# Tiles at equal places modulo 2 KB, one 1/rms chain for two row tiles, and the first bias tiles loaded ahead, in a fp32r transformer block

## The chip, the cores and the metric

The kernel runs on one core of one Trainium2 chip. The metric is the device time of one execution in microseconds, as the median of several runs. The core has a tensor engine (TensorE, PE in the profile; its weight loads are PEld), a vector engine (VectorE, DVE), a scalar engine (ScalarE, ACT), GpSimd (POOL) and a queue engine (SyncE, SP) that issues nearly all DMA transfers here, in order. Each engine works through its own instructions in order and waits on semaphores.

## The reference, cut to what matters

One layer of an encoder with 1024 positions and width 1024: attention over chunks, a short convolution, gates, an output projection and an MLP.

```python
h = rms_norm(x, norm1_g)
q, k, v, bg, cg, xc = split(h @ w_in)                     # 6 x 1024 columns
y_attn = attention(rms_norm(q), rms_norm(k), v, rel_bias) @ w_attn_proj   # 16 heads of 64
y_conv = (bg * conv3(cg * xc)) @ w_conv_proj
g_attn, g_conv = split(sigmoid(h @ w_gate + b_gate))
x = x + (g_attn * y_attn + g_conv * y_conv) @ w_out
x = x + square(relu(rms_norm(x, norm2_g) @ w_up)) @ w_down
```

## The kernel before

Every fp32 matrix product is done as three fp32r products: an operand is cut into a high part (ScalarE, a cast) and a low part (VectorE, the difference), and high x high, low x high and high x low are added in PSUM. `split` does the cut. A step of a product is thus three matmuls, mostly with 128x128 stationary tiles and 512 moving columns.

**The start and the first pair of heads.** The positions are eight row tiles of 128. `row_load` fetches a transposed row tile `xt`, `row_cut` multiplies it with the gain and cuts it into `hT` (row tiles 0 to 3 in `hT0`, 4 to 7 in `hT1`). `row_scale` fetches the same rows in the other layout (`xn`), and ScalarE and GpSimd make 1/rms of the rows (`rr`) from them. For head pair `p`, `fetch` and `cut` load and cut four weight tiles (`r_q`, `w_q`); then each row tile takes 24 matmuls into `psq` (q, k and v of two heads, 384 columns). `evac` empties it: ScalarE squares (`sq`), VectorE adds up (`ss`, the reduction), GpSimd makes 1/rms of each head (six small instructions on tile `qw`, the function `rstd` among them), VectorE multiplies (`qn`). The last step is put off by `later(QN[0], ...)`, and so are the values `vt`. After row tile 5, `tr_q` and `tr_k` transpose the first four row tiles of q and k (`tq`, `tk`), cut them (`qh`, `kh`), and copies by DMA make `q` and `k2` of them. In the first pair the `psq` tiles go round eight PSUM banks, three of which `tq` and `tk` use too.

**Attention.** For each pair `unit_stages` makes scores `s` (PSUM), adds the bias tile `b` and finds the largest (L361, VectorE), exponentiates, transposes (`tp`), cuts (`pt`) and multiplies with `vt` (`av`). The next pair's 192 `psq` matmuls are woven in between. `load_bias` fetches a bias tile and masks two corners on GpSimd. The bias tiles lie in pool `a2`, which is opened on the right side of SBUF after `ln1`, the pool of the start, is closed.

**Seven-product jobs.** The gates 4 to 7 of eight, the convolution's projections and the up projection run as jobs of two by two blocks with seven products (`product`, `phase`): each of the seven block products of a job is 4 steps of 3 matmuls with 512 columns, 84 matmuls in a job. There are 16 such jobs before the projections and 16 in the up projection. In each set the first job is "wide" (all seven products for one moving tile after the other), the last is wide too, in the order `leave`; the 14 between are regular: each product goes through its four moving tiles, three matmuls each. The moving tiles are `oh0` to `oh3` and `on0` to `on3`, one after the other.

**Plain stages.** `ps_cp`, `ps_ap`, `ps_o` and `ps_d` (the convolution's and attention's projections, the output projection, and the down projection) are products of 512 columns in PSUM with all weights on the right side of SBUF. Their moving tiles are `yk`, `ak`, `mk` and `uk`.

**SBUF** is given out from two sides: pools by default from the left (low addresses), those with `side="right"` from the right. The left side begins behind a scratch area that the compiler keeps for DMA descriptors.

Of the kernel before, what the change touches and what calls it, by code (L numbers as in the profile page):

```python
# [40 lines left out]
def block_kernel(ctx, tc, x, xt, wqkv, wcnv, wgate, wcp, wap, wout, wup, wdown,  # L41
# [14 lines left out]
    make_identity(nc, ident)  # L56
    ones = const.tile([P, P], F32, name="ones")
    nc.gpsimd.memset(ones[:], 1.0)
    nhalf = const.tile([P, 4], F32, name="nhalf")
    nc.gpsimd.memset(nhalf[:], -0.5)  # L60
    gq8 = const.tile([P, 1], F32, name="gq8")
    nc.vector.tensor_scalar(gq8[:], sv[:, C_GQ:C_GQ + 1], DH ** -0.5, None, op0=ALU.mult)
# [109 lines left out]
    uD = [dram.tile([P, S], F32, name=f"uD{t}") for t in range(FF // P)]  # L172


    def row_load(pool, st, parts=1):
        xg = pool.tile([P, ND, P], F32, name=f"xt{st}", tag="xt", bufs=4)
        n = ND // parts
        for i in range(parts):
            nc.sync.dma_start(xg[:, i * n:(i + 1) * n], xt[st, :, i * n:(i + 1) * n])
        return xg  # L180

    def row_cut(xg, st, parts=1, gated=False):
        so = (st % 4) * P
        h = hT[st // 4]
        n = ND // parts
        for i in range(parts):
            k = slice(i * n, (i + 1) * n)
            g = sv[:, C_G1 + i * n:C_G1 + (i + 1) * n].unsqueeze(2).to_broadcast([P, n, P])
            ins = (nc.vector.tensor_tensor(xg[:, k], xg[:, k], g, op=ALU.mult),)
            ins += split(h[:, 0, k, so:so + P], h[:, 1, k, so:so + P], xg[:, k])  # L190
            if gated:
                for j in ins:
                    gate(j)

    def row_scale(pool, sts):
        n, a = len(sts), sts[0]
        w = pool.tile([P, 4, 4], F32, name=f"rw{a}", tag="rw")
        ss, v, y, t = (w[:, i, :n] for i in range(4))
        for st in sts:
            xn = pool.tile([P, D], F32, name=f"xn{st}", tag="xn")  # L200
            nc.sync.dma_start(xn[:], x[st * P:(st + 1) * P, :])
            nc.scalar.activation(xn[:], xn[:], AF.Square, accum_out=w[:, 0, st - a:st - a + 1])
        nc.gpsimd.tensor_scalar(v, ss, 1.0 / D, EPS, op0=ALU.mult, op1=ALU.add)
        nc.gpsimd.tensor_scalar(rr[:, 1, a:a + n], v, EPS, None, op0=ALU.mult)
        rstd(y, t, v)
        nc.gpsimd.tensor_scalar(t, t, -0.5, 1.5, op0=ALU.mult, op1=ALU.add)
        nc.gpsimd.tensor_tensor(rr[:, 0, a:a + n], y, t, op=ALU.mult)
# [7 lines left out]
    def qkv_stages(p):  # L215
# [39 lines left out]
        def evac(st, ps):  # L255
            hf, s4 = st // 4, st % 4
            qk = ps[:, 0:256].rearrange("p (a b) -> p a b", a=4)
            sq = aw.tile([P, 4, DH], F32, name=f"sq{p}_{st}", tag="sq")
            w = a1.tile([P, 4, 4], F32, name=f"qw{p}_{st}", tag="qw")
            ss, v, y, t = (w[:, i, :] for i in range(4))  # L260
            nc.scalar.square(sq[:], qk)
            nc.vector.tensor_reduce(ss, sq[:], axis=AX.X, op=ALU.add)

            nc.gpsimd.tensor_scalar(v, ss, 1.0 / DH, rr[:, 1, st:st + 1], op0=ALU.mult, op1=ALU.add)
            rstd(y, t, v)
            nc.gpsimd.tensor_scalar(t, t, -0.5, 1.5, op0=ALU.mult, op1=ALU.add)
            nc.gpsimd.tensor_tensor(y, y, t, op=ALU.mult)
            pv = ps[:, 256:384].rearrange("p (h d) -> p h d", h=2)
            vh, vl = c.vt[:, st, :, 0, :], c.vt[:, st, :, 1, :]
            r = rr[:, 0, st:st + 1]  # L270

            def values():
                gate(nc.scalar.activation(vh, pv, AF.Copy, scale=r))
                gate(nc.vector.scalar_tensor_tensor(vl, pv, r, vh.bitcast(F32),
                                                    op0=ALU.mult, op1=ALU.subtract))

            def normed():
                gate(nc.vector.tensor_tensor(
                    c.qn[hf][:, s4].rearrange("p a (h d) -> p (a h) d", h=2),
                    qk, y.unsqueeze(2).to_broadcast([P, 4, DH]), op=ALU.mult))  # L280
# [46 lines left out]
    biast = {}

    def load_bias(p, h):
        if p >= NH // 2:  # L330
            return
        bt = biast[p, h] = a2.tile([P, 5 * P], F32, name=f"b{p}_{h}", tag="bias")
        nc.sync.dma_start(bt[:], biasw[2 * p + h])
        nc.gpsimd.memset(bt[0:64, 576:640], NEG)
        nc.gpsimd.memset(bt[64:128, 0:64], NEG)

    def unit_stages(p, c, m, h):

# [115 lines left out]
            later(n, lambda f=f, u=u: f(u))  # L454


    QN, VN = [7], [7]
    pairs = [qkv_stages(p) for p in range(NH // 2)]
    cur, fetch, cut, tiles, trs = pairs[0]
    with tc.tile_pool(name="ln1", bufs=2) as ln1:  # L460
        xs = {0: row_load(ln1, 0, 2)}
        for u in range(4):
            fetch(u, ln1 if u < 2 else None)
        xs[1] = row_load(ln1, 1)
        row_cut(xs[0], 0, 2)
# [24 lines left out]
        turn[0] = 0  # L490
        banks = [(psmm, "mm")] * 2
# [598 lines left out]
```

## Time and profile before

| | |
|---|---|
| median of 3 runs | 1859.92 us (1859.12 to 1860.83) |
| profiled execution | 1858.92 us, span 1857.1 us |
| TensorE busy | 97% of the span, 8884 matmuls |
| VectorE busy | 61% |
| ScalarE busy | 38% |
| GpSimd busy | 9% |
| mean granted TensorE clock | 0.989 |

The profile is of one execution; its times are microseconds from the first instruction. A busy TensorE is not one at its peak: the matmuls are pipelined, so that a matmul's own duration overlaps the next one's, and how fast they follow each other has to be read from the starts. In a timeline, instructions of one line and tile that follow each other are one row: start, length, and how many (x). What stands in brackets is the engine's idle time before the row and what ended it.

### The profile page before, as it was taken

To read this page: it belongs to the slowest core of one execution; us is meant where nothing else is said; L and a number is where in the kernel's file an instruction comes from. 1 tells how busy PE (TensorE), PEld (TensorE's weight loads), DVE (VectorE), ACT (ScalarE), POOL (GpSimd) and SP (SyncE) were. 2 spreads that over 40 slices of the span, in tenths; PEclk is the share of its full clock that TensorE was granted. 3 is DMA by queue.
4 is the path that set the end of the run, shared out by engine and by line. 5 is a ranking of instruction groups with operands and counts; after the bars stand their busy time and mean duration, and the time that the engine had idled before them with its cause. 6 is when DMAs were issued, how large, how long until landed. Compare 5 with 4: busy or idle time off the path is not lost.

```text
span 1857.1 us, 24757 instructions
## 1 busy us (share of the span) xinstructions
PE 1808.5 (97%) x8884; PEld 1549.0 (83%) x8884; DVE 1124.4 (61%) x2068; ACT 698.2 (38%) x1337; POOL 163.4 (9%) x463
## 2 busy tenths in 40 slices
PE   7899999999999999999999999999999989999998
PEld 6799999999887788888788888788788868888887
DVE  6578787787658766665651528966676451423343
ACT  5455555565433433333341414433333242312210
POOL 5433233222100000000000000000000000000000
PEclk9999999999999899999999999999999999999999
DMA  6433434333425232223583528543233262424232
GB/s 250 117 100 100 104 93 111 103 103 93 115 77 167 80 98 79 63 69 102 187 265 109 178 83 266 190 131 114 94 113 120 91 220 69 131 66 132 68 111 82
DMA packets 123547, 225.02 MB, mean 121 GB/s; under 512 B 13728, under 2 KB 30112, under 8 KB 123424
## 3 DMA queue, kind: packets, MB, share of 16 engines
q1 hardware_dynamic: 123280, 223.40, 39.3%
q8 instruction: 70, 1.15, 0.3%
q14 instruction: 53, 0.43, 0.1%
q10 hardware_dynamic: 144, 0.03, 0.0%
HBM read 147.88 MB, written 50.33 MB: 107 GB/s over the span
## 4 chain that ended last, share of the span: by engine, by line
PE 89%; DVE 4%; DMA 2%; POOL 2%; issue 1%; ACT 1%; SPq 0%; DVEq 0%; ACTq 0%
PE ps_d L74 19%; PE psq L74 12%; PE pa_u L74 8%; PE ps_ap L74 5%; PE ps_o L74 5%; PE ps_cp L74 4%; PE pb_u L74 4%; PE av L74 3%; PE s L74 3%; PE ps_g L74 3%; PE tp L77 3%; PE pa_c L74 2%; PE pa_x L74 2%; PE pa_b L74 2%; PE pc_u L74 2%; PE pa_g L74 1%
## 5 line engine op out<-in xcount | busy, mean ns | idle before, releaser
L74 PE MATMUL psq<-w_q,hT 128*128 128x384 f32 x1536 | 348.6, 352 | 9.9 <-ACT w_q L81 7.3
L74 PE MATMUL ps_d<-uk,w_d 128*128 128x512 f32 x1536 | 351.2, 391 | 6.6 <-DVE uk L82 5.5
L74 PEld LDWEIGHTS ps_d<-uk,w_d 128*128 128x128 f32 x1536 | 289.9, 189 | 67.8 <-DVE uk L82 5.9
L74 PEld LDWEIGHTS psq<-w_q,hT 128*128 128x128 f32 x1536 | 262.8, 193 | 13.6 <-ACT w_q L81 7.3
L74 PE MATMUL pa_u<-on,w_u 128*128 128x512 f32 x672 | 162.9, 394 | 0.0
L74 PEld LDWEIGHTS pa_u<-on,w_u 128*128 128x128 f32 x672 | 126.2, 188 | 29.5 <-issue 0.5
L82 DVE TENSOR_TENSOR w_d<-r_d,w_d 128x512 fp32r<-128x512 f32 x64 | 43.3, 690 | 148.7 <-ACT w_d L81 148.7
L363 ACT ACTIVATE p<-p,sm 128x640 f32<-128x640 f32 (+4 forms) x128 | 89.5, 699 | 83.6 <-DVE sm L361 83.6
L81 ACT CAST w_d<-r_d 128x512 fp32r<-128x512 f32 x64 | 39.2, 623 | 178.5 <-PE ps_d L74 173.3
L74 PE MATMUL ps_g<-hT,w_g 128*128 128x512 f32 x384 | 100.2, 398 | 1.4 <-DVE gp L521 1.4
L74 PE MATMUL ps_cp<-yk,w_cp 128*128 128x512 f32 x384 | 90.4, 398 | 4.5 <-DVE yk L82 3.8
L361 DVE CUSTOM_DVE_ANT_0 p<-s,b 128x640 f32<-128x640 f32 (+4 forms) x128 | 83.4, 652 | 13.7 <-PE s L74 10.4
L74 PEld LDWEIGHTS ps_cp<-yk,w_cp 128*128 128x128 f32 x384 | 73.8, 193 | 20.9 <-DVE yk L82 4.2
L82 DVE TENSOR_TENSOR pt<-tp,pt 128x512 fp32r<-128x512 f32 (+1 forms) x144 | 84.4, 597 | 11.1 <-ACT pt L81 10.5
L74 PE MATMUL s<-k,q 128*128 128x384 f32 (+3 forms) x384 | 82.0, 322 | 6.6 <-DVE sm L361 6.2
L74 PEld LDWEIGHTS av<-pt,vt 128*128 128x128 f32 x576 | 85.5, 188 | 3.2 <-DVE pt L82 1.2
L74 PE MATMUL ps_ap<-ak,w_ap 128*128 128x512 f32 x384 | 88.1, 391 | 0.0
L74 PE MATMUL av<-pt,vt 128*128 128x256 f32 (+1 forms) x576 | 86.7, 272 | 1.0 <-DVE pt L82 1.0
L74 PE MATMUL ps_o<-mk,w_o 128*128 128x512 f32 x384 | 87.3, 389 | 0.0
L81 ACT CAST pt<-tp 128x512 fp32r<-128x512 f32 (+1 forms) x144 | 71.7, 515 | 40.2 <-PE tp L77 40.0
L74 PEld LDWEIGHTS ps_ap<-ak,w_ap 128*128 128x128 f32 x384 | 72.1, 188 | 15.8
L74 PEld LDWEIGHTS ps_o<-mk,w_o 128*128 128x128 f32 x384 | 72.1, 188 | 15.0
(244 smaller groups left out, 2908.6 us busy)
## 6 DMA issues: line engine op xcount, KB each, us to landing
q<-qh SPq DMA_DIRECT2D x128, 128.0 KB, 2.3
r_u_a<-in_wup_dram SPq DMA_DIRECT2D x64, 256.0 KB, 2.7
buk<-uD SPq DMA_DIRECT2D x32, 512.0 KB, 3.7
r_d<-in_wdown_dram SPq DMA_DIRECT2D x64, 256.0 KB, 2.8
r_q<-in_wqkv_dram SPq DMA_DIRECT2D x32, 384.0 KB, 3.4
k<-kh SPq DMA_DIRECT2D x64, 128.0 KB, 2.3
gl<-gD SPq DMA_DIRECT2D x32, 256.0 KB, 3.5
uD<-s_u SPq DMA_DIRECT2D x30, 256.0 KB, 2.0
```

The source lines that it names most:

```text
L74: pin(nc.tensor.matmul(ps, lhsT, rhs, start=start, stop=stop, skip_group_check=chain))
L77: pin(nc.tensor.transpose(o, i, ident[:]))
L81: return (nc.scalar.copy(hi, src), nc.vector.tensor_tensor(lo, src, hi.bitcast(F32), op=ALU.subtract))
L82: nc.vector.tensor_tensor(lo, src, hi.bitcast(F32), op=ALU.subtract))
L361: nc.vector.tensor_tensor_reduce(pw, sc[:, k0:k1], biast[p, h][:, 5 * P - w:], -1.0, 3e38, ALU.add, ALU.min, sm[:, 0:1])
L363: nc.scalar.activation(pw, pw, AF.Exp, bias=sm[:, 0:1], scale=-1.0, accum_out=sm[:, 1:2])
```

## The change

It has three parts.

1. **Places.** The DMA scratch area is set to 1 KB (16 KB before), and a tile `pad` that nothing uses is put on the left side. The built program's addresses, as bytes past a multiple of 2 KB:

| tiles | side | before | after |
|---|---|---|---|
| `hT`, `w_q`, `w_g` 0 to 4, `vt`, `qn` | left | 1568, and steps of 512 | 2016, and steps of 512 |
| `oh1` to `oh3`, `on0`, `on1`, `ak` | left | 1568 | 2016 |
| weights `w` of all later stages | right | 2016, and steps of 512 | the same |
| `oh0`, `on2`, `on3`, `yk`, `mk`, `uk` | right | 2016 | the same |
| `pt` | right | 992 | 992 |
| `q`, `k2` | left | 1696 | 1184 |

2. **One chain for two row tiles.** In the first pair (`p == 0`) `evac` collects the sums of two row tiles in one tile `qw` and runs the chain from `rstd` on once for both, on eight columns. `normed` of the even row tile is put off by eight steps more. `vt` comes nine steps later instead of seven.
3. **Loads and cuts ahead.** The bias tiles of pair 0 move to pool `a1` on the left and are loaded after row tile 2. The loads of the first `xt` and `r_q` alternate in halves, and so do their cuts; the first two `r_q` share the buffers of `xn`.

```diff
-    nhalf = const.tile([P, 4], F32, name="nhalf")
+    nhalf = const.tile([P, 8], F32, name="nhalf")
...
-        raw = (pool or wp[0]).tile([P] + shape, F32, name=f"r_{name}", tag="raw",
-                                   bufs=2 if pool else wp[2])
+        raw = (pool or wp[0]).tile([P] + shape, F32, name=f"r_{name}",
+                                   tag="xn" if pool else "raw", bufs=2 if pool else wp[2])
...
+    const.tile([P, 368], F32, name="pad")
...
+        bt = biast[p, h] = a1.tile([P, 5 * P], F32, name=f"b{p}_{h}", tag="bias")
...
-            w = a1.tile([P, 4, 4], F32, name=f"qw{p}_{st}", tag="qw")
-            ss, v, y, t = (w[:, i, :] for i in range(4))
+            n = 2 if p == 0 else 1
+            b, m = st % n, st - st % n
+            if b == 0:
+                c.qw = a1.tile([P, 3, 4 * n], F32, name=f"qw{p}_{st}", tag=f"qw{n}")
+            w = c.qw
+            ss, v, y = (w[:, i, 4 * b:4 * b + 4] for i in range(3))
...
-            rstd(y, t, v)
-            nc.gpsimd.tensor_scalar(t, t, -0.5, 1.5, op0=ALU.mult, op1=ALU.add)
-            nc.gpsimd.tensor_tensor(y, y, t, op=ALU.mult)
+            if b == n - 1:
+                va, ya, ta = (w[:, i, :] for i in (1, 2, 0))
+                rstd(ya, ta, va)
+                nc.gpsimd.tensor_scalar(ta, ta, -0.5, 1.5, op0=ALU.mult, op1=ALU.add)
+                nc.gpsimd.tensor_tensor(ya, ya, ta, op=ALU.mult)
...
-            later(QN[0], normed)
+            later(QN[0] + 8 * (n - 1 - b), normed)
...
-    QN, VN = [7], [7]
+    QN, VN = [7], [9]
...
-        xs = {0: row_load(ln1, 0, 2)}
-        for u in range(4):
-            fetch(u, ln1 if u < 2 else None)
+        xs = {0: row_load(ln1, 0, 2, lambda i: [fetch(u, None if i else ln1)
+                                                for u in (2 * i, 2 * i + 1)])}
         xs[1] = row_load(ln1, 1)
-        row_cut(xs[0], 0, 2)
-        for u in range(4):
-            cut(u, False)
+        row_cut(xs[0], 0, 2, False, lambda i: [cut(u, False) for u in (2 * i, 2 * i + 1)])
...
+            if st == 2:
+                for h in range(2):
+                    load_bias(0, h)
...
-    for h in range(2):
-        load_bias(0, h)
...
-    nc = _bacc.Bacc("TRN2", target_bir_lowering=False, num_devices=1)
+    nc = _bacc.Bacc("TRN2", target_bir_lowering=False, num_devices=1,
+                     dynamic_dma_scratch_size=1024)
```

How the instructions stand on two engines. VectorE at the start of the program, before (L189 multiplies `xt` with the gain, L82 makes the low part; L262 is the reduction of row tile 0):

```order
L189 TENSOR_TENSOR xt_197<-xt_197,sv 128x512 x2
L82 TENSOR_TENSOR hT_76<-xt_197,hT_76 128x4x128 x2
L82 TENSOR_TENSOR w_q_0_216<-r_q_0_200,w_q_0_216 128x768
L82 TENSOR_TENSOR w_q_1_219<-r_q_1_202,w_q_1_219 128x768
L82 TENSOR_TENSOR w_q_2_222<-r_q_2_204,w_q_2_222 128x768
L82 TENSOR_TENSOR w_q_3_225<-r_q_3_206,w_q_3_225 128x768
L189 TENSOR_TENSOR xt_208<-xt_208,sv 128x1024
L82 TENSOR_TENSOR hT_76<-xt_208,hT_76 128x8x128
L189 TENSOR_TENSOR xt_242<-xt_242,sv 128x1024
```

The same place now (`xt_198` is row tile 0, `xt_209` row tile 1, `xt_243` row tile 2):

```order
L193 TENSOR_TENSOR xt_198<-xt_198,sv 128x512
L82 TENSOR_TENSOR hT_76<-xt_198,hT_76 128x4x128
L193 TENSOR_TENSOR xt_198<-xt_198,sv 128x512
L82 TENSOR_TENSOR w_q_0_214<-r_q_0_200,w_q_0_214 128x768
L82 TENSOR_TENSOR w_q_1_217<-r_q_1_202,w_q_1_217 128x768
L82 TENSOR_TENSOR hT_76<-xt_198,hT_76 128x4x128
L82 TENSOR_TENSOR w_q_2_223<-r_q_2_205,w_q_2_223 128x768
L82 TENSOR_TENSOR w_q_3_226<-r_q_3_207,w_q_3_226 128x768
L193 TENSOR_TENSOR xt_209<-xt_209,sv 128x1024
L193 TENSOR_TENSOR xt_243<-xt_243,sv 128x1024
L82 TENSOR_TENSOR hT_76<-xt_209,hT_76 128x8x128
```

The second half of row tile 0 now stands between the weights, and the low part of row tile 1 has moved behind the product of row tile 2.

GpSimd at the chains of row tiles 2 and 3, before (L264 is the chain's first instruction, L114 its power, L267 its last):

```order
L264 TENSOR_SCALAR qw_3_457<-qw_3_457,rr 128x4
L114 TENSOR_TENSOR qw_3_457<-qw_3_457,nhalf 128x4
L115 TENSOR_TENSOR qw_3_457<-qw_3_457 128x4
L116 TENSOR_TENSOR qw_3_457<-qw_3_457 128x4
L266 TENSOR_SCALAR qw_3_457<-qw_3_457 128x4
L267 TENSOR_TENSOR qw_3_457<-qw_3_457 128x4
```

The same place now (L285 is the old L264, L222 and L223 mask a bias tile, `qw_2_390` holds row tiles 2 and 3):

```order
L222 MEMSET b_0_399 64x64
L223 MEMSET b_0_399 64x64
L285 TENSOR_SCALAR qw_2_390<-qw_2_390,rr 128x4
L114 TENSOR_TENSOR qw_2_390<-qw_2_390,nhalf 128x8
L222 MEMSET b_1_403 64x64
L223 MEMSET b_1_403 64x64
L115 TENSOR_TENSOR qw_2_390<-qw_2_390 128x8
L116 TENSOR_TENSOR qw_2_390<-qw_2_390 128x8
L289 TENSOR_SCALAR qw_2_390<-qw_2_390 128x8
L290 TENSOR_TENSOR qw_2_390<-qw_2_390 128x8
```

One chain on eight columns stands for two on four, and the bias masks have come from behind row tile 7's chain into this one.

VectorE around the first `qn`, now (L297 is the low part of `vt`, L301 is `qn`, `xt_266` is row tile 4 and `xt_259` row tile 3):

```order
L193 TENSOR_TENSOR xt_266<-xt_266,sv 128x1024
L82 TENSOR_TENSOR hT_76<-xt_259,hT_76 128x8x128
L283 TENSOR_REDUCE qw_0_294<-sq_1_342 128x4
L297 SCALAR_TENSOR_TENSOR vt_261<-psq_0_263,rr,vt_261 128x2x64
L82 TENSOR_TENSOR hT_77<-xt_266,hT_77 128x8x128
L301 TENSOR_TENSOR qn_0_262<-psq_0_263,qw_0_294 128x256
L301 TENSOR_TENSOR qn_0_262<-psq_1_298,qw_0_294 128x256
```

Before, `qn` of row tiles 0 and 1 stood ahead of the low part of row tile 4; now both stand behind it.

## Rows read from the trace of the kernel before

**Rows 1.** The page, TensorE: busy us, share of the span, instructions.

```profile
PE 1808.5 (97%) x8884; PEld 1549.0 (83%) x8884; DVE 1124.4 (61%) x2068; ACT 698.2 (38%) x1337; POOL 163.4 (9%) x463
```

**Rows 2.** Timelines of TensorE in `ps_d`, `ps_o`, `ps_ap`: start, length, engine, count.

```profile
1699.62 50.71 PE L74 MATMUL ps_d<-uk,w_d 128*128 128x512 f32 x223
...
1109.69 40.51 PE L74 MATMUL ps_o<-mk,w_o 128*128 128x512 f32 x178
...
1039.80 40.45 PE L74 MATMUL ps_ap<-ak,w_ap 128*128 128x512 f32 x176
```

**Rows 3.** Timelines of TensorE in regular up jobs and in regular convolution jobs.

```profile
1216.78 5.71 PE L74 MATMUL pa_u<-on,w_u 128*128 128x512 f32 x24
...
1255.61 5.71 PE L74 MATMUL pa_u<-on,w_u 128*128 128x512 f32 x24
...
651.05 2.96 PE L74 MATMUL pa_x<-oh,w_x 128*128 128x512 f32 x12
...
695.58 2.96 PE L74 MATMUL pc_x<-oh,w_x 128*128 128x512 f32 x12
```

**Rows 4.** Timelines of TensorE within the last up job, two stretches.

```profile
1475.03 8.32 PE L74 MATMUL p_u<-on,w_u 128*128 128x512 f32 x36
...
1484.35 8.40 PE L74 MATMUL p_u<-on,w_u 128*128 128x512 f32 x36
```

**Rows 5.** Windows: length, then busy us (count) of PE, PEld, DVE, ACT, POOL, clock.

```profile
620.00:880.00 260.00, 260.00 (x1123) 210.90 (x1122) 166.22 (x240) 89.68 (x148) 0.31 (x3) 1.00 0.27 82
1190.00:1468.00 278.00, 274.45 (x1183) 221.50 (x1182) 185.66 (x280) 92.39 (x162) 0.00 (x0) 1.00 0.34 112
...
80.00:560.00 480.00, 478.03 (x3094) 455.39 (x3093) 361.37 (x946) 262.46 (x629) 119.72 (x352) 1.00 0.38 101
```

**Rows 6.** Timelines of TensorE in the first 80 us.

```profile
8.28 19.63 PE L74 MATMUL psq<-w_q,hT 128*128 128x384 f32 x97 [0.30 <-DVE w_q L82]
29.59 6.70 PE L74 MATMUL psq<-w_q,hT 128*128 128x384 f32 x37 [1.69 <-DVE hT L82]
...
42.17 0.47 PE L77 MATMUL tq<-ident,qn 128*128 128x128 f32 x1 [3.99 <-DVE qn L278]
...
44.77 9.73 PE L74 MATMUL psq<-w_q,hT 128*128 128x384 f32 x46 [0.62 <-DVE hT L82]
...
62.91 0.79 PE L74 MATMUL s<-k,q 128*128 128x256 f32 x2 [5.93 <-DVE sm L361]
63.51 5.56 PE L74 MATMUL psq<-w_q,hT 128*128 128x384 f32 x18
```

**Rows 7.** Windows: the stretch after the longest wait (third from the end: granted clock).

```profile
63.40:68.20 4.80, 4.80 (x17) 4.80 (x17) 1.90 (x8) 0.89 (x4) 0.00 (x0) 0.50 0.02 3
```

**Rows 8.** Timeline of all engines in 34 to 75.

```profile
37.51 1.95 POOL L264 TENSOR_SCALAR qw<-qw,rr 128x4 f32<-128x4 f32 x1 [0.89 <-DVE qw L262]
...
41.70 0.42 DVE L278 TENSOR_TENSOR qn<-psq,qw 128x256 f32<-128x256 f32 x1 [2.03 <-POOL qw L267]
...
56.35 0.81 SPq L333 DMA_DIRECT2D b<-in_biasw_dram  x2
...
62.56 0.29 DVE L361 CUSTOM_DVE_ANT_0 p<-s,b 128x128 f32<-128x128 f32 x1 [2.87 <-POOL b L334]
```

**Rows 9.** Groups of GpSimd in 14 to 63: count, busy us, mean ns, idle before.

```profile
L114 POOL TENSOR_TENSOR qw<-qw,nhalf 128x4 f32<-128x4 f32 x8 | 9.0, 1128 | 0.6
L264 POOL TENSOR_SCALAR qw<-qw,rr 128x4 f32<-128x4 f32 x8 | 6.5, 817 | 3.2 <-DVE qw L262 2.7
```

**Rows 10.** Timeline of all engines in 0 to 34.

```profile
4.22 1.35 DVE L189 TENSOR_TENSOR xt<-xt,sv 128x512 f32<-128x512 f32 x2
...
7.52 2.77 ACT L81 CAST w_q<-r_q 128x768 fp32r<-128x768 f32 x3 [0.29 <-DMA r_q<-in_wqkv_dram]
...
8.38 2.90 DVE L82 TENSOR_TENSOR w_q<-r_q,w_q 128x768 fp32r<-128x768 f32 x3 [0.16 <-ACT w_q L81]
...
13.53 1.23 DVE L82 TENSOR_TENSOR hT<-xt,hT 128x1024 fp32r<-128x1024 f32 x1 [1.11 <-ACT hT L81]
```

More of the change, by code (lines that the diff above doesn't have):

```diff
@@ L172, in block_kernel, with row_load @@
     uD = [dram.tile([P, S], F32, name=f"uD{t}") for t in range(FF // P)]
-    def row_load(pool, st, parts=1):
+    def row_load(pool, st, parts=1, then=None):
         xg = pool.tile([P, ND, P], F32, name=f"xt{st}", tag="xt", bufs=4)
@@ L179, in row_load, with row_cut @@
             nc.sync.dma_start(xg[:, i * n:(i + 1) * n], xt[st, :, i * n:(i + 1) * n])
+            if then:
+                then(i)
         return xg
-    def row_cut(xg, st, parts=1, gated=False):
+    def row_cut(xg, st, parts=1, gated=False, then=None):
         so = (st % 4) * P
@@ L193, in row_cut @@
                     gate(j)
+            if then:
+                then(i)
     def row_scale(pool, sts):
@@ L207, in row_scale, with load_bias @@
         nc.gpsimd.tensor_tensor(rr[:, 0, a:a + n], y, t, op=ALU.mult)
+    biast = {}
+    def load_bias(p, h):
+        if p >= NH // 2:
+            return
+        bt = biast[p, h] = a1.tile([P, 5 * P], F32, name=f"b{p}_{h}", tag="bias")
+        nc.sync.dma_start(bt[:], biasw[2 * p + h])
+        nc.gpsimd.memset(bt[0:64, 576:640], NEG)
+        nc.gpsimd.memset(bt[64:128, 0:64], NEG)
     PA = [slice(0, DH), slice(DH, P)]
@@ L325, in skip @@
         pass
[L327 to L335, printed above, removed]
     def unit_stages(p, c, m, h):
```

## The prediction

> **What bounds the kernel now.** I read the page first: TensorE is busy 97% of the span [rows 1], so the time can fall in two ways only: its idle time goes, or its matmuls follow each other faster. The matmuls' own durations overlap and hide the second, so I took TensorE's timeline in stretches without a wait and divided: (length of the merged row − 0.39, the last matmul's own duration) / (count − 1) is the step from one start to the next. All matmuls below are 128x512 fp32r with a 128x128 stationary tile and the same three products per step.
>
> - `ps_d`: (50.71 − 0.39)/222 = 226.7 ns; `ps_o`: (40.51 − 0.39)/177 = 226.7 ns. `ps_ap`: (40.45 − 0.39)/175 = 228.9 ns [rows 2].
> - The seven-product jobs: 14 products of 12 between the two rows of the up projection, 38.83 us/168 = 231.1 ns; 16 products in the convolution's jobs, 44.53/192 = 231.9 ns [rows 3].
>
> The work per instruction is equal, so why three steps? By the table of places above, `ps_d` and `ps_o` read weights and moving tile both at 2016 past a multiple of 2 KB; `ps_ap` reads weights at 2016 and moving tile at 1568; the seven-product jobs read moving tiles that change between 1568 and 2016 every three to nine matmuls. Two other readings would fit so far (the stage, or the seven-product code), so I looked for the same code without the change of side: the last up job (`leave` = 2, 3, 0, 1) reads 42 matmuls from right tiles and then 42 from left ones. The first stretch goes at (8.32 − 0.39)/35 = 226.6 ns, the second at (8.40 − 0.39)/35 = 228.9 ns [rows 4]. Same code, tiles, weights; only the place differs. I take it that equal places give 226.7, unequal ones 228.9, and a change of place now and then some ns more. TensorE is the bound in these stages: in 620 to 880 it is busy all 260 us, VectorE 166; in 1190 to 1468 274 of 278, VectorE 186 [rows 5].
>
> Then the idle time. The first 80 us hold most of TensorE's waits [rows 6]: 1.69 us at 29.59 for `hT`, 3.99 at 42.17 for `qn`, 0.62 at 44.77, 5.93 at 62.91 for `sm`. The two long ones cost twice: after them the granted clock is at its half level (0.50, 1.2 GHz) for 63.4 to 68.2 [rows 7], and the 18 matmuls from 63.51 take 5.56 us, where full speed, 0.176 by the row from 29.59 ((6.70 − 0.35)/36), gives 17 × 0.176 + 0.35 = 3.35.
>
> Who is late there? VectorE runs in order. `qn` at 41.70 waited 2.03 us for GpSimd, whose chain for that row tile began at 37.51 and took L264 alone 1.95 us; only after `qn` comes the next reduction [rows 8]. So each row tile pays reduction, GpSimd chain, `qn` in series. The mean chain is 0.82 + 1.13 for L264 and L114 [rows 9] and four short ones. And 62.91 waits for the bias: its load is issued at 56.35, since its tile takes the place of `ln1`'s last tiles, and VectorE stands 2.87 us until it is masked [rows 8].
>
> **Part by part.**
>
> 1. *Places.* 28 regular seven-product jobs of 84 matmuls, half of them up: 1176 × (231.1 − 226.7) = 5.2 us and 1176 × (231.9 − 226.7) = 6.1 us. The four wide jobs have 42 + 42 + 63 + 63 = 210 matmuls on left tiles: 210 × 2.2 = 0.5. `ps_ap`: 384 × 2.2 = 0.85. Sum 12.7 us, all of it on the path, because VectorE has the room above. Lower bound 0 (the place is not the cause), upper bound 2688 × 5.2 + 0.85 = 14.8 (the wide jobs too). I take 12.7, the stretches being so regular.
> 2. *Attention.* `vt` moves from 1568 to 2016 and so agrees modulo 512 with `pt` at 992, `k2` and `q` with each other as before. No row separates this: TensorE is busy 478.03 of 480 us there over 3094 matmuls [rows 5]. The 576 `av` matmuls could gain at most the 4.4 ns of part 1, 2.5 us; at least, places that now differ elsewhere take back as much, −2.5. I take 0.5.
> 3. *Pair chain.* Two L264, one L114 of eight columns and four short ones replace two whole chains; L114 costs between one of 1.13 and two, 2.26; I take 1.7. VectorE stops once in two row tiles and no longer between `sq` and the next reduction. In the new VectorE order `hT` of tile 4 stands ahead of both `qn`, so the 1.69 goes: 1.7 us. For `tq`: from the start of the wait, 38.18, to the end of tile 7, 54.50, are 16.3 us; the work in it is 48 × 0.176 for tiles 6 and 7 and some 0.6 for five transposes (an estimate: 128 of 384 columns are 0.059, twice that each) = 9.0. Gain 7.3, if the second chain ends before TensorE has done tile 5. Tile 1 counts from 16.05 (part 5), each tile is 24 × 0.176 = 4.2: tile 3 ends at 28.7, its square and reduction at 29.5 (an estimate: two of the 0.42 of `qn`). Then L264 0.82, L114 1.7, the short ones with their gaps 1.1 (41.70 − 37.51 − 1.95 − 1.13) and some 0.6 for four bias masks: 33.7; both `qn` by 34.6; TensorE reaches `tq` at 16.05 + 5 × 4.2 = 37.1. So 2.5 us to spare. Next late are `hT` of tile 6 (34.6 + 0.4 + 1.23 + 1.23 = 37.5, wanted at about 38) and the `q` and `k` copies, for which I find no spare time: up to 1 us of wait.
>    The even tile's `qn` comes eight steps later and holds its bank; the bank is wanted five tiles later, so the matmuls of the tiles between cover it.
> 4. *Bias ahead.* The wait of 5.93 and the slow clock after it go: 5.93 + (5.56 − 3.35) = 8.1 us. What it adds: two loads in SP's queue behind the first two `r_q` of pair 1, and four masks on GpSimd inside the second chain. Behind a mask that waits for its load stand the chain, both `qn`, `tq`. At a late load each us beyond the 2.5 to spare is one of TensorE's.
> 5. *The new start.* The second half of `xt0` now lands behind two weight loads, at about the time that the second of these did, 7.5 [rows 10]. VectorE needs it before `w_q`: 7.5 + 0.68 + 0.97 = 9.15 for the second matmul, against 8.28. Then come `w_q` 1, half of `hT`, `w_q` 2 and 3 (0.97, 0.69, 0.97, 0.97) and, as the order shows, `xt1`, `xt2` and only then `hT` of tile 1 (1.23 each): 16.4 against 13.53 + 1.23 = 14.76. TensorE's tile 1 began at 27.91 − 0.35 − 73 × 0.176 = 14.7 and wants this at its third matmul, 15.05: a loss of 1.3 us. If the loads land earlier than I think it is 0; if `xt2`'s load holds VectorE, some 2.5. The shared `xn` ring makes SP wait for `w_q` 0 (9.15) before `xn0`, and behind it stand `xt2` and the rest; `xn0` feeds a chain that is not wanted before tile 1 is done, so the 4.2 us of tile 1 cover it.
>
> Sum: 12.7 + 0.5 + 1.7 + 7.3 + 8.1 − 1.3 = 29.0 us. The profiled execution took 1858.92, 1.0 below the median of the runs, 1859.92; its span of 1857.1 should become 1828. For the median: **1830.9, I say 1830.5**.
>
> **Rivals.** What this kernel's runs can tell from no change is about 0.2%, 3.7 us.
>
> - *Places do nothing* (the step belongs to the stage). Then part 1 is gone: 1830.5 + 12.7 = 1843. For it: `ps_ap` is another stage than `ps_d`. Against it: the two stretches of one job [rows 4].
>   The Trainium skill, "TensorE: Matmul & The Clock Gate", Part 2 (step ①), has TensorE read the moving tile and the next weights through two independent ports, the load taking nothing from the running matmul. By this rule where the tiles stand would not matter, and the result would be this rival's 1843. The 2.3 ns between the stretches of [rows 4] disagree with it, so it gets a small chance.
> - *The pair chain stalls TensorE again.* In before, L264 took 0.82 on average but 1.95 once. If the chain and the masks take 7 us instead of 4, `tq` waits again, long enough for the half clock, and part 3's 7.3 and perhaps a us of part 4 are lost: 1836 to 1840.
> - *Slower.* The half clock stays. TensorE's start now has one matmul at about 6.5 and then a hole until 9.15, and feeds that are just in time. Each matmul at 1.2 GHz costs (5.56 − 3.35)/17 = 0.13 us more. To eat the 29 us and come out 3.7 slower takes 33/0.13 = 254 of them, more than the first pair's 192; time 1863.6 or more. Against it: the slow stretch from 63.51 ended within 18 matmuls.
> - *Rather more*: no loss at the start, and 2.5 from attention: 1827.
>
> **How the numbers follow.** Both gains as summed, ± 1 us in parts 1 and 2, from −1 to +3 in 3 to 5: 1827.5 to 1834, 68%. Chain stalls: 18%. More: 5%. Places do nothing: 7%. Slower: 1%; nearly no change, from two of these together: 1%. The range of 1825 to 1839 takes in the first, the "more" and most of the stalls. Faster by over 0.2%: 0.97; same 0.01; slower 0.02.
>
> **What would show it.** Part 1: products of the up and convolution jobs start every 2.72 us instead of 2.77 to 2.80, and `ps_ap` merges to 226.7. Part 3: no wait of TensorE on `qn`, none on `hT` over 1.5 us, and a granted clock of 1.00 from 17 us on. Part 4: no wait on `sm` at the second score tile. Part 5: the second matmul at 9.2, and tile 1's third at 16.4. I would be wrong if the products still start every 2.77, if GpSimd's eight-column L114 is well over 2.3 us, or if a mask waits for its load.

## The result, and the profile after

The changed kernel takes 1838.44 us (median of 4 runs, 1836.54 to 1842.08) against 1859.89 before: a ratio of 0.9887, 95% interval 0.9869 to 0.9904, so 21 us faster. The forecast was 1830.5, with a range of 1825 to 1839: the sign and the range hold, the size is 7.9 us short. That the range holds is in part luck: the time lies 0.6 us inside its upper end, and the same kernel run once more took 1840.76 (run 11 below). The profiled execution took 1839.77 us, its span is 1838.0.

Timelines of TensorE in the changed kernel, for [rows 2 to 4]: products of regular convolution and up jobs, `ps_ap`, and the last up job.

```profile
641.73 2.88 PE L74 MATMUL pa_x<-oh,w_x 128*128 128x512 f32 x12
644.45 2.88 PE L74 MATMUL pa_b<-oh,w_b 128*128 128x512 f32 x12
...
999.81 40.51 PE L74 MATMUL ps_ap<-ak,w_ap 128*128 128x512 f32 x178
...
1213.28 2.88 PE L74 MATMUL pb_u<-on,w_u 128*128 128x512 f32 x12
1216.00 2.88 PE L74 MATMUL pa_u<-on,w_u 128*128 128x512 f32 x12
...
1454.40 19.20 PE L74 MATMUL p_u<-on,w_u 128*128 128x512 f32 x84
```

These stages now have one step: 2.72 us for a product of twelve in both sets of jobs, (40.51 − 0.39)/177 = 226.7 ns in `ps_ap`, and (19.20 − 0.39)/83 = 226.6 in the last job, which before fell into a stretch of 226.6 and one of 228.9. This half of the change did what was forecast. The first 80 us did not. TensorE there, for [rows 6], and its granted clock after the two waits, third column from the end, for [rows 7]:

```profile
9.29 7.02 PE L74 MATMUL psq<-w_q,hT 128*128 128x384 f32 x25 [2.04 <-DVE w_q L82]
17.17 20.74 PE L74 MATMUL psq<-w_q,hT 128*128 128x384 f32 x118 [0.85 <-DVE hT L82]
40.58 0.63 PE L77 MATMUL tq<-ident,qn 128*128 128x128 f32 x4 [2.67 <-DVE qn L301]
43.76 1.08 PE L77 MATMUL tk<-ident,qn 128*128 128x128 f32 x4 [2.56 <-DVE vt L297]
44.50 10.52 PE L74 MATMUL psq<-w_q,hT 128*128 128x384 f32 x48
54.85 0.34 PE L74 MATMUL s<-k,q 128*128 128x128 f32 x2
...
56.64 0.40 PE L74 MATMUL s<-k,q 128*128 128x256 f32 x2
```

```profile
44.50:54.80 10.30, 10.30 (x50) 10.30 (x49) 5.61 (x11) 5.15 (x11) 6.74 (x21) 0.80 0.74 171
```

The wait of 5.93 us on `sm` is gone, and so is the one for `hT` of tile 4. But `tq` still waits 2.67 us for `qn`, behind it `tk` waits 2.56 us for `vt`, which nothing had forecast, and then the clock falls: 48 matmuls take 10.52 us where full speed gives 8.6 (run 9 below). The first score starts at 54.85. In the kernel before it started at 54.90:

```profile
54.90 0.42 PE L74 MATMUL s<-k,q 128*128 128x128 f32 x2 [0.40 <-DMA k<-kh]
```

So in these two executions nothing of the start's gain has come by the first score, and all of it comes behind it.

What holds `qn` is seen in the timeline of the other engines, for [rows 8]:

```profile
25.52 0.27 POOL L285 TENSOR_SCALAR qw<-qw,rr 128x4 f32<-128x4 f32 x1
25.87 1.64 POOL L114 TENSOR_TENSOR qw<-qw,nhalf 128x8 f32<-128x8 f32 x1
...
28.68 0.76 DVE L301 TENSOR_TENSOR qn<-psq,qw 128x256 f32<-128x256 f32 x2 [3.31 <-POOL qw L290]
...
29.53 0.37 ACT L296 ACTIVATE vt<-psq,rr 128x128 fp32r<-128x128 f32 x1 [2.65 <-DVE qn L301]
29.68 1.22 DVE L193 TENSOR_TENSOR xt<-xt,sv 128x1024 f32<-128x1024 f32 x1
29.86 1.17 POOL L285 TENSOR_SCALAR qw<-qw,rr 128x4 f32<-128x4 f32 x1 [0.94 <-DVE qw L283]
...
32.17 1.12 POOL L115 TENSOR_TENSOR rw<-rw 128x2 f32<-128x2 f32 x1
32.62 0.38 ACT L282 ACTIVATE sq<-psq 128x256 f32<-128x256 f32 x1
...
34.02 0.41 DVE L283 TENSOR_REDUCE qw<-sq 128x4 f32<-128x256 f32 x1
...
35.74 1.08 POOL L285 TENSOR_SCALAR qw<-qw,rr 128x4 f32<-128x4 f32 x1
...
39.77 0.20 POOL L290 TENSOR_TENSOR qw<-qw 128x8 f32<-128x8 f32 x1
40.01 0.76 DVE L301 TENSOR_TENSOR qn<-psq,qw 128x256 f32<-128x256 f32 x2 [3.31 <-POOL qw L290]
```

Row tile 3 leaves TensorE at 17.17 + 70 × 0.174 = 29.4, but its square (32.62) and reduction (34.02) are late: VectorE stood 3.31 us ahead of the first pair of `qn`, and ScalarE's `vt` of tile 1 waited for that same `qn` (2.65). Behind `vt` on ScalarE stand the cut of a row tile, which waits for VectorE's product from 29.68, and a weight cut, and only then the square. Then GpSimd has the rows' own 1/rms (`rw`) to finish; it takes the second chain up at 35.74, and the chain ends at 39.97.

### The profile page after: what moved, and what is told of

The parts are those of the page before. It is cut to its first block, busy times and chain, and to the rows that moved or that the text cites. A ratio compares the mean times of both kernels' runs of the same rounds, so it can differ in the third digit from the quotient of the medians.

```text
span 1838.0 us, 24737 instructions
## 1 busy us (share of the span) xinstructions
PE 1793.2 (98%) x8884; PEld 1545.9 (84%) x8884; DVE 1124.0 (61%) x2068; ACT 698.1 (38%) x1337; POOL 158.8 (9%) x443
## 4 chain that ended last, share of the span: by engine, by line
PE 90%; DVE 5%; DMA 2%; POOL 1%; issue 1%; ACT 1%; SPq 0%; DVEq 0%; ACTq 0%
PE ps_d L74 19%; PE psq L74 13%; PE pa_u L74 8%; PE ps_ap L74 5%; PE ps_o L74 5%; PE ps_cp L74 4%; PE pb_u L74 4%; PE av L74 3%; PE s L74 3%; PE ps_g L74 3%; PE tp L77 3%; PE pa_c L74 2%; PE pa_b L74 2%; PE pa_x L74 2%; PE pc_u L74 2%; PE p_g L74 1%
## 5 line engine op out<-in xcount | busy, mean ns | idle before, releaser
L82 DVE TENSOR_TENSOR w_d<-r_d,w_d 128x512 fp32r<-128x512 f32 x64 | 43.3, 690 | 148.8 <-ACT w_d L81 148.8
L82 DVE TENSOR_TENSOR pt<-tp,pt 128x512 fp32r<-128x512 f32 (+1 forms) x144 | 84.4, 597 | 10.6 <-ACT pt L81 9.6
```

What stands on the lines that cost most here:

```text
L82: nc.vector.tensor_tensor(lo, src, hi.bitcast(F32), op=ALU.subtract))
```

## The experiments

Since the work after the first pair scatters by some 4 us between the profiled executions (last section), each kernel is also read at one event: the first of the `rb` matmuls, which comes when the start is over. In three profiled executions with the changed kernel's start it came at 82.05, 81.28 and 80.95, so a difference of about 1 us there says nothing.

| kernel | ratio to before, 95% interval | median us | first `rb` matmul |
|---|---|---|---|
| before | | 1859.89 | 90.13 |
| changed | 0.9887 (0.9869 to 0.9904) | 1838.44 | 82.05 |
| 1 places only | 0.9932 (0.9918 to 0.9945) | 1846.91 | 90.18 |
| 2 no places | 0.9959 (0.9946 to 0.9971) | 1851.96 | 83.19 |
| 3 `vt` at seven | 0.9891 (0.9877 to 0.9904) | 1839.31 | 79.49 |
| 4 `qn` later | 0.9883 (0.9870 to 0.9897) | 1837.52 | 80.31 |
| 5 pad 512 less | 0.9889 (0.9874 to 0.9904) | 1841.39 | 81.28 |
| 6 places and bias | 0.9907 (0.9892 to 0.9921) | 1843.60 | 86.23 |
| 7 single chain | 0.9898 (0.9881 to 0.9914) | 1842.35 | 85.76 |
| 8 chain on VectorE | 0.9879 (0.9865 to 0.9894) | 1837.90 | 79.94 |
| 9 the same, six tiles | 0.9867 (0.9852 to 0.9882) | 1836.24 | 76.80 |
| 10 and cuts later | 0.9871 (0.9855 to 0.9888) | 1837.20 | 80.37 |
| 11 changed, again | 0.9893 (0.9879 to 0.9908) | 1840.76 | 80.95 |
| 12 as 9, old start | 0.9882 (0.9865 to 0.9898) | 1838.40 | 80.66 |

Runs 1 to 4, runs 5 to 8, runs 9 to 11 and run 12 shared the kernel before; its medians were 1859.69, 1861.01, 1860.58 and 1861.02, so across these groups the ratios are compared.

**1. Places only.** The kernel before with the scratch area and the pad:

```diff
+    const.tile([P, 368], F32, name="pad")
...
+                     dynamic_dma_scratch_size=1024)
```

> The kernel before with the 1 KB scratch area and the pad, nothing else. Theory (equal places are worth the steps that the changed kernel's trace shows: 6.1 us in the convolution jobs, some 3.5 to 5 in the up jobs, 0.9 in the attention projection, about 0.5 in the wide jobs): 1847 to 1849 us. Rival (the gain of the change lies in its start alone): 1859 to 1861 us. The wait on sm of 5.9 us and the one on qn of 4 us in the first pair stay as in the kernel before, by both.

Measured: 12.8 us less than before, and `rb` where it was. The sum of part 1 was 12.7. No run has the smaller scratch area without the pad. That the places do it and not the scratch area is read from the kernel before: with 16 KB `ps_d` and `ps_o` went at 226.7 ns [rows 2]. Nor is it the place 2016 in itself: in the kernel before the last gates (`ps_g`) read `hT` and weights both on the left, at 1568:

```profile
553.69 32.89 PE L74 MATMUL ps_g<-hT,w_g 128*128 128x512 f32 x144 [1.45 <-DVE gp L521]
```

(32.89 − 0.39)/143 = 227.3 ns, so two tiles at 1568 go as fast as two at 2016.

**2. No places.** The changed kernel without these two lines.

> The changed kernel with the scratch area of before and without the pad: the start's changes alone. Theory (start and places add up): 1838.4 + 11 to 12.7 = 1849 to 1851.5 us, with up and convolution products back at 2.77 to 2.80 us each. Rival (the start's gain is given back later, or needs the places): 1855 us or more.

Its timeline of TensorE in an up job:

```profile
1214.36 2.94 PE L74 MATMUL pc_u<-on,w_u 128*128 128x512 f32 x12
1217.13 2.94 PE L74 MATMUL pa_u<-on,w_u 128*128 128x512 f32 x12
```

The products are back at 2.77. The time, 1851.96, lies just above what was expected; the two halves multiply, 0.9932 × 0.9959 = 0.9891, to the ratio of the whole within its interval. So places and start are independent as far as this can tell, and the start is worth 7.7 us, not 16.3 with the attention.

**3. `vt` at seven steps**, in place of nine:

```diff
-    QN, VN = [7], [9]
+    QN, VN = [7], [7]
```

> The changed kernel with vt seven steps after its row tile, as before, in place of nine. Theory A (with nine, the vt copy of each odd row tile stands behind its own qn on ScalarE, and holds the squares behind it and the bank that tk needs): the 2.56 us wait of TensorE ahead of tk goes, and some of the half clock after it: 1834 to 1836.5 us; the wait ahead of tq, 2.67 us, shrinks only if VectorE's reduction of row tile 3 comes earlier than 34.0. Theory B (the order of vt costs nothing; VectorE and GpSimd alone set tq and tk): 1838 to 1839 us and both waits stay over 2 us.

TensorE in this run:

```profile
39.46 0.83 PE L77 MATMUL tq<-ident,qn 128*128 128x128 f32 x4 [2.41 <-DVE qn L301]
40.12 0.60 PE L77 MATMUL tk<-ident,qn 128*128 128x128 f32 x4
...
52.97 0.42 PE L74 MATMUL s<-k,q 128*128 128x128 f32 x2 [1.79 <-DMA k<-kh]
```

Theory A is right on the mechanism: the wait ahead of `tk` is gone, and `rb` comes 1.5 to 2.6 us earlier. The executions also differ in when their first matmuls start, which has nothing to do with `vt`: counted from the third matmul of tile 1 (16.30 here; 17.17, 16.21 and 16.80 in the three above) it is 1.0 to 1.9. The median, 1839.31, doesn't show it, within an interval of ± 2.5 us. Part of the gain went into a new wait: `s` now waits 1.79 us for the copy of `k`. And `tq` is as late as before, so `vt` was not what held it.

**4. `qn` of the first four row tiles four steps later**, on top of run 3:

```diff
-            later(QN[0] + 8 * (n - 1 - b), normed)
+            later(QN[0] + 8 * (n - 1 - b) + 4 * (p == 0 and st < 4), normed)
```

> As the run with vt at seven steps, and qn of the first four row tiles four steps later, so that VectorE does the reduction of row tile 2 before it stands and waits for the first chain. Theory A (VectorE's stop of 3.3 us ahead of the first qn, with the reductions behind it, makes the second chain late): the reduction of row tile 3 comes at about 32 in place of 34.0, the wait ahead of tq falls from 2.67 us to under 1.7, and the time is 1 to 3 us below the run with vt at seven. Theory B (GpSimd itself is late, with the chain of the rows' own 1/rms and its stretched instructions): the wait ahead of tq stays over 2.3 us and the time is that of the run with vt at seven.

The timeline around the second chain, GpSimd and TensorE:

```profile
34.61 1.06 POOL L116 TENSOR_TENSOR rw<-rw 128x2 f32<-128x2 f32 x1
...
36.61 0.27 POOL L285 TENSOR_SCALAR qw<-qw,rr 128x4 f32<-128x4 f32 x1
36.96 2.68 POOL L114 TENSOR_TENSOR qw<-qw,nhalf 128x8 f32<-128x8 f32 x1
...
41.38 0.87 PE L77 MATMUL tq<-ident,qn 128*128 128x128 f32 x3 [3.42 <-DVE qn L301]
```

Theory A fell by its waits. The reduction came at 33.20, 0.8 us earlier than in the changed kernel, but GpSimd took it up only at 36.61, when it was through with `rw`, and its power took 2.68. The wait grew to 3.42. The median, 1837.52, is 1.8 us below run 3's as theory A has it, but inside both intervals.

**5. A pad 512 bytes shorter:**

```diff
-    const.tile([P, 368], F32, name="pad")
+    const.tile([P, 240], F32, name="pad")
```

> The changed kernel with a pad shorter by 512 bytes: the left tiles then begin 1504 past a multiple of 2 KB, equal to the right tiles' 2016 modulo 512 but not modulo 2 KB. Theory A (what counts is the place modulo 512, since the weights themselves already stand at 2016 and steps of 512 from it at the same step of 226.7 ns): the time and the products of the changed kernel, 1838 to 1839 us, 2.72 us for a product. Theory B (modulo 2 KB, as the change is named): products at 2.75 to 2.80 us, 1847 to 1850 us.

TensorE in this run:

```profile
999.80 40.51 PE L74 MATMUL ps_ap<-ak,w_ap 128*128 128x512 f32 x178
```

The left tiles are now 512 bytes off the right ones modulo 2 KB, and the steps don't change: 226.7 ns here, and 2.72 us for a product of the convolution jobs. So places need not be equal modulo 2 KB; equal modulo 512 is enough (1568 and 2016 are 32 and 480; 1504 and 2016 are both 480). Modulo 256 or 128 would fit these runs as well, since 1568 and 2016 differ by 448 bytes; modulo 64 would not, as 448 is a multiple of it. The median, 1841.39, is above the 1838 to 1839 of theory A, but the ratio, 0.9889, is the changed kernel's (0.9887).

**6. Places and bias.** Run 1, and the bias tiles in `a1`, loaded after row tile 2:

```diff
-        bt = biast[p, h] = a2.tile([P, 5 * P], F32, name=f"b{p}_{h}", tag="bias")
+        bt = biast[p, h] = a1.tile([P, 5 * P], F32, name=f"b{p}_{h}", tag="bias")
...
+            if st == 2:
+                for h in range(2):
+                    load_bias(0, h)
```

> The kernel before with the places and the bias tiles loaded ahead into the left pool, without the pair chain, the new order of the start and vt at nine steps. Theory A (of the start's three changes the bias alone pays: 5.93 us of wait and 2.2 of half clock; the pair chain and the new start give and take nothing): 1846.9 - 8.1 = 1838.8 us, within 1.5 us of the changed kernel; the waits on hT and qn of the kernel before stay. Theory B (the pair chain is worth what the prediction says, less the waits on tq): 1841 us or more.

Its timeline at the second score tile:

```profile
59.16 0.42 DVE L291 TENSOR_TENSOR qn<-psq,qw 128x256 f32<-128x256 f32 x1 [2.96 <-POOL qw L280]
...
59.83 0.28 DVE L364 CUSTOM_DVE_ANT_0 p<-s,b 128x128 f32<-128x128 f32 x1
...
60.17 0.80 PE L74 MATMUL s<-k,q 128*128 128x256 f32 x2 [2.43 <-DVE sm L364]
```

The bias is there, and the wait is still 2.43: the first score's step on VectorE stands behind a `qn` that waits 2.96 us for its chain. Alone the bias is worth 0.0025 of the time, 4.7 us (4.0 at `rb`), not 8.1, and the time, 1843.60, is that of theory B.

**7. Single chain.** Run 3 with a chain for each row tile:

```diff
-            n = 2 if p == 0 else 1
+            n = 1
```

> As the run with vt at seven steps, with a chain for each row tile as before. Theory A (one chain for two tiles saves no more GpSimd time than it makes VectorE wait): within 1.5 us of the run with vt at seven, 1838 to 1840.5 us, and a wait ahead of tq of 2 to 4 us. Theory B (the pair chain is what brings tq forward): TensorE's waits ahead of tq and for hT add up to over 5 us, and the time is 1842 us or more.

TensorE in this run:

```profile
41.98 0.33 PE L77 MATMUL tq<-ident,qn 128*128 128x128 f32 x1 [3.88 <-DVE qn L301]
...
44.57 10.87 PE L74 MATMUL psq<-w_q,hT 128*128 128x384 f32 x46 [1.48 <-DVE hT L82]
...
59.48 0.51 PE L74 MATMUL s<-k,q 128*128 128x256 f32 x2 [2.23 <-DVE sm L374]
```

Theory B: the waits for `qn` and `hT` add up to 5.36, and the time is 1842.35. With the pair chain (run 3) `rb` comes 6.3 us earlier: 2.3 of them by the first score (55.27 here, 52.97 there) and 4.0 behind it, where run 3 has no wait on `sm` and this run has one of 2.23 with the bias long loaded. The medians show less, 0.0007 or 1.3 us, inside both intervals; this run's profile is its longest execution and run 3's its shortest. So the pair chain pays, between these two figures; which is nearer stays open. Against run 6 this run has the new start, and nothing else that moves an instruction there: 0.5 us at `rb`, less than that event scatters.

**8. The chain's short steps on VectorE**, on top of run 3; the power stays on GpSimd:

```diff
+            e = nc.vector if p == 0 else nc.gpsimd
-            nc.gpsimd.tensor_scalar(v, ss, 1.0 / DH, rr[:, 1, st:st + 1], op0=ALU.mult, op1=ALU.add)
+            e.tensor_scalar(v, ss, 1.0 / DH, rr[:, 1, st:st + 1], op0=ALU.mult, op1=ALU.add)
...
-                rstd(ya, ta, va)
+                rstd(ya, ta, va, e)
```

> [...] Theory A (GpSimd is the late engine: each of its short steps that starts during a VectorE product ends only with that product, 0.8 to 1.2 us in place of 0.2, and the rows' own 1/rms stands ahead of the second chain): the second pair of qn starts at 37.5 or earlier in place of 38.9, the wait ahead of tq is under 1.3 us, and the time 1 to 3 us below the run with vt at seven. Theory B (the waits between the two engines set it, whichever runs the steps): the wait stays over 2 us and the time is that of the run with vt at seven.

VectorE ahead of the second pair of `qn`, and TensorE at `tq` and at the second score tile:

```profile
36.08 0.17 DVE L115 TENSOR_TENSOR qw<-qw 128x8 f32<-128x8 f32 x1 [1.53 <-POOL qw L114]
...
36.90 1.22 DVE L193 TENSOR_TENSOR xt<-xt,sv 128x1024 f32<-128x1024 f32 x1
...
38.11 1.22 DVE L82 TENSOR_TENSOR hT<-xt,hT 128x1024 fp32r<-128x1024 f32 x1
39.24 0.75 DVE L302 TENSOR_TENSOR qn<-psq,qw 128x256 f32<-128x256 f32 x2
39.81 0.63 PE L77 MATMUL tq<-ident,qn 128*128 128x128 f32 x4 [2.27 <-DVE qn L302]
...
54.95 0.50 PE L74 MATMUL s<-k,q 128*128 128x256 f32 x2 [2.39 <-DVE sm L375]
```

GpSimd hands its power over at 36.0, 2.8 us before its chain ended in run 3, and yet `qn` comes at 39.24 and `tq` still waits 2.27 us: now two row cuts of 1.22 us stand between the chain's last steps and `qn` on VectorE. Theory A's signs (`qn` by 37.5, a wait under 1.3) failed: relieving GpSimd alone does not bring `tq` forward. The time, 0.9879 against run 3's 0.9891, is inside both intervals. At the second score the wait on `sm` is back, because the score's step stands behind the last chain on VectorE.

**9. The same for row tiles 0 to 5 alone:**

```diff
-            e = nc.vector if p == 0 else nc.gpsimd
+            e = nc.vector if p == 0 and st < 6 else nc.gpsimd
```

> As the run with the chain's short steps on VectorE, but for row tiles 0 to 5 alone; the last two keep theirs on GpSimd. Theory A (the 2.39 us that TensorE waited for sm in that run came from VectorE, where the first score's steps stood behind the last chain's power): that wait goes, and the start ends 2 to 3 us earlier, some 1834 to 1836 us. Theory B (the score waits for something else): the wait stays.

TensorE in this run:

```profile
40.11 0.63 PE L77 MATMUL tq<-ident,qn 128*128 128x128 f32 x4 [2.19 <-DVE qn L302]
...
40.93 8.60 PE L74 MATMUL psq<-w_q,hT 128*128 128x384 f32 x48
50.24 0.42 PE L74 MATMUL s<-k,q 128*128 128x128 f32 x2 [0.71 <-DMA k<-kh]
...
52.13 0.40 PE L74 MATMUL s<-k,q 128*128 128x256 f32 x2
```

Theory A: the wait on `sm` is gone, the 48 matmuls go at full clock (8.60), and `rb` comes 4.2 us ahead of run 11, the changed kernel beside it. The medians on that chip are 1836.24 and 1840.76, and the executions don't overlap (1833.75 to 1837.32; 1840.47 to 1841.10). This kernel beats the changed one.

**10. Run 9, with two weight cuts later:**

```diff
-        for n, u, f in ((18, 0, fetch), (18, 1, fetch), (24, 0, cut), (32, 1, cut),
-                        (38, 2, fetch), (38, 3, fetch), (60, 2, cut), (62, 3, cut)):
+        for n, u, f in (((18, 0, fetch), (18, 1, fetch), (40, 0, cut), (42, 1, cut),
+                         (44, 2, fetch), (44, 3, fetch), (60, 2, cut), (62, 3, cut))
...
```

> As the run before it in this list, and the next pair's first two weight cuts moved from steps 24 and 32 to 40 and 42, behind qn of row tiles 2 and 3 on VectorE. Theory A (VectorE, with these two cuts of 0.95 us and the cuts of two row tiles ahead of that qn, is what keeps tq waiting): qn of row tiles 2 and 3 comes at 37.5 or earlier in place of 39.2, the wait ahead of tq is under 1 us, the granted clock stays full, and the time is 1831 to 1834.5 us. Theory B (the row cuts of tiles 6 and 7 are late next): a wait for hT of 1 to 2.5 us takes the place of the wait ahead of tq, 1834 to 1837 us.

TensorE in this run:

```profile
38.78 0.33 PE L77 MATMUL tq<-ident,qn 128*128 128x128 f32 x1 [0.41 <-DVE qn L302]
...
51.48 0.66 PE L74 MATMUL s<-k,q 128*128 128x128 f32 x2 [3.61 <-DMA k<-kh]
```

The wait ahead of `tq` falls to 0.41, as theory A has it, and the gain is lost again at `s`, which waits 3.61 us for the copy of `k`; neither theory had that place, and the time, 1837.20, is outside what both gave. ScalarE takes `qh` up at 42.45 (40.97 in run 9), and SP needs 5.2 us to issue the eight copies of `q` ahead of those of `k`.

**11. The changed kernel again**, beside runs 9 and 10.

> The changed kernel itself, beside the two above on one chip. Theory: 1836 to 1842 us as before, with the waits ahead of tq and tk of 2.5 us each; what differs between its executions lies in matmuls at half clock after waits of about 3 us, not in the steps of the stages, which stay at 226.7 ns.

1840.76 us, with the same two waits (2.67 and 2.10).

**12. Run 9 with the old start:** the loads and cuts of the first row tile in the order of the kernel before.

```diff
-        row_cut(xs[0], 0, 2, False, lambda i: [cut(u, False) for u in (2 * i, 2 * i + 1)])
+        row_cut(xs[0], 0, 2)
+        for u in range(4):
+            cut(u, False)
...
```

> As the run with the chain's short steps on VectorE for row tiles 0 to 5, with the loads and cuts of the first row tile and weights in the order of the kernel before. Theory A (the new order costs TensorE's first matmuls about as much as it gives later, so that it is worth nothing within 1.5 us): the second matmul at 8.5 to 8.8 in place of 9.3 to 9.9, no wait at the third matmul of tile 1, the wait ahead of tq longer by what the matmuls gained, and 1834.5 to 1838 us. Theory B (the old order makes hT of tile 4 late again, behind the first qn): a wait of about 2 us for hT at 27 to 30, part of it ahead of tq as well, and 1838 us or more.

TensorE in this run:

```profile
29.96 8.27 PE L74 MATMUL psq<-w_q,hT 128*128 128x384 f32 x46 [1.83 <-DVE hT L82]
...
42.63 1.09 PE L77 MATMUL tq<-ident,qn 128*128 128x128 f32 x4 [4.40 <-DVE qn L302]
```

Theory B by its waits: `hT` of tile 4 is late again by 1.83, and `tq` waits 4.40. At `rb` the new start is worth 3.9 us here; by the medians 0.0015, 2.8 us, with intervals that overlap.

## Why the prediction was right, and 7.9 us short

**Places (12.7).** Right, term by term: run 1 measures 12.8. In the profiles the convolution jobs (from the first start of `pa_c` to the last of `pa_g`) take 266.48 us for 272.54, a gain of 6.1 as forecast; `ps_ap`, first to last start, 86.81 for 87.68. The up jobs take 272.91 for 276.36, which is 1.7 short of the 5.2: in this profile the granted clock was 0.72 in 1187 to 1193, after a wait (last section). In run 1, where it stayed at 1.00 there, they take 271.24, and the 5.1 us are there. The rival "places do nothing" falls with run 1. The Trainium skill, "TensorE: Matmul & The Clock Gate", Part 2 (step ①), says that loading the next weights takes no read bandwidth from the running matmul. What the prediction drew from it, that the places would not matter, disagrees with the 226.7 and 228.9 to 231.9 ns measured; whether the two reads are what collides no run shows.

**Attention (+0.5).** From `rb` to the first `ps_g` matmul it took 380.70 us before and 381.07 now, so −0.4; small, and not followed up.

**The start (1.7 + 7.3 + 8.1 − 1.3 = 15.8).** It gave 8.1 by `rb` (90.13 to 82.05). The first score parts the sum. Ahead of it 1.7 + 7.3 − 1.3 = 7.7 were forecast, and 0.05 came (54.90 to 54.85; 0.8 and 1.1 by the same kernel's start in runs 5 and 11). Behind it 8.1 were forecast, and 8.0 came (35.23 us from the first score to `rb` before, 27.20 now). So what the forecast lacks was lost ahead of the first score: `tq` waits 2.67, `tk` 2.56, and the lower clock costs 1.9, together 7.1 of part 3's 7.3. Two steps failed there, and one behind it came true for another reason than the one given.

- *The second chain, "33.7; both `qn` by 34.6".* It ended at 39.97. Its length was right, 4.2 us with the masks (35.74 to 39.97); its beginning was wrong. The sum began with a reduction done at 29.5, as soon as TensorE was through. But VectorE stood ahead of the first `qn` until 28.68, and what waited for it on ScalarE and VectorE put the square and the reduction of row tile 3 off, so that the reduction ended at 34.43. Another 1.3 us went to GpSimd, which had the rows' own 1/rms to finish; its short steps take 0.79 to 1.12 us where they run beside VectorE's products, and the sum left them out. Neither is alone what holds `tq`: in run 4 the reduction came earlier, in run 8 GpSimd was relieved, and `tq` waited 3.42 and 2.27. Only with GpSimd relieved and two weight cuts out of VectorE's way (run 10) did the wait fall to 0.41.
- *`vt` at nine steps.* It got no price. With `qn` of odd row tiles at seven, `vt` falls behind it on the same bank, and `tk`, which takes such a bank, waited 2.56. Run 3 shows that two steps make this wait, worth 1.0 to 1.9 us at `rb`. The sentence that the matmuls between cover the bank held for the tiles and not for `tk`.
- *Bias, 8.1.* The number came, the reason was half of it. The step took all of TensorE's wait of 5.93 for the bias's share. [Rows 8] had the right number: VectorE stood 2.87 us for the mask, and the other 3.06 lay in what stood ahead of that on VectorE, a `qn` that waits for its chain. Run 6 shows it: with the bias there the wait is 2.43, and the bias alone is worth 4.7. The rest goes with the pair chain, as run 3 against run 7 shows. No run has the pair chain without the bias ahead.

The pair chain itself was priced too high: 7.3 forecast ahead of the first score, 2.3 there in run 3 against run 7, and between 1.3 (medians) and 6.3 (`rb`) in all. The new start was −1.3 with 1.7 for `hT`, so +0.4: 0.5 in run 7 against run 6, which is within the scatter, more in run 12, where nothing else is late. The second matmul came at 9.29 (9.15 forecast), tile 1's third at 17.17 (16.4).

So of the rivals "the pair chain stalls TensorE again" (18%, 1836 to 1840) is what happened in place, clock and time: `tq` waits, at 0.80 of the clock after it. Its reason was another: the chain and the masks took not 7 us but 4.2, and the eight-column power 1.64, near the 1.7 taken; they began late, because of what stands ahead of them in three queues.

## What to carry to other kernels

Read what a wait is worth from the engine that is waited for: its own idle time on that releaser, not the whole wait at the far end; the rest has another cause that is late next, and goes only if that goes too. In a loop over two engines in order, list every instruction that stands between the links on each of them, those of other chains too, before pricing one link. For matmuls that follow each other without a wait, allocate the moving tiles and weights at the same place modulo 512 bytes (shown here for 128x512 fp32r): it cost two lines and gave more than half of the gain here.

## What the runs showed of the hardware that was not expected

- **Place modulo 512.** Moving tile and weights at equal places modulo 512 give 226.7 to 227.3 ns a step for 128x512 fp32r matmuls; 448 bytes apart, the one other distance that was run, they give 228.9, and 231.1 to 231.9 where the moving tile's place changes every few matmuls (kernel before, runs 1, 2, 5). Why, no run shows.
- **GpSimd beside VectorE.** The same 128x4 instruction (L285) took 0.27 us alone and 1.17 when it began just after a VectorE product of 1.22 us, and ended with it (31.03 and 30.90). So did L115, 0.20 us at 45.95 beside no such product: 1.12 at 32.17 (to 33.29, VectorE's product to 33.24). The Trainium skill, "SBUF — State Buffer", section "Who interferes with whom", says that a VectorE instruction with two inputs in SBUF contends with a GpSimd instruction that reads SBUF, since VectorE's second input comes through the read interface that the two share. These products have two such inputs, and the trace agrees. A mean such as the 0.82 of [rows 9] hides these two cases.
- **A 3 us hole and the clock.** At the start of the up jobs TensorE waits for `w_u`, 2.85 us in run 1 and 2.89 in run 9. In run 1 the clock stayed full after it, in run 9 it didn't; windows after that wait of run 1 and of run 9 (third column from the end):

```profile
1195.20:1203.00 7.80, 7.80 (x35) 6.45 (x36) 6.80 (x12) 2.35 (x4) 0.00 (x0) 1.00 0.86 290
```

```profile
1183.30:1191.00 7.70, 7.70 (x21) 6.10 (x22) 6.74 (x11) 1.76 (x3) 0.00 (x0) 0.61 0.79 280
```

  35 matmuls in 7.80 us against 21 in 7.70. From `rb` to the end of the span the kernels with equal places took 1754.4 us (runs 8 and 12) to 1758.7 (run 9): such stretches come and go from one profile to the next, and gains of 2 us at the start are hard to see in a median. What decides it after nearly the same wait was not found.
